# Shifting the split weight tiles by 0, 64, 128 or 192 bytes, and four raw buffers instead of five

## The chip, the cores and the metric

The kernel runs on one core of one Trainium2 chip. The metric is the device time of one execution in microseconds (us). Before the change the median of three runs is 472.22 us, from 471.35 to 472.73.

## The reference

One decoder layer for 256 tokens of width 2048, all in float32. `x` is normalized, multiplied by a weight `w_in` (2048 x 8192), and the product is cut into eight groups of 1024 columns. Four of them feed a gated convolution of width 3, four feed attention with 8 heads of 128. The two results are normalized, gated, joined and multiplied by `w_out` (2048 x 2048).

```
h = rms_norm(x, norm_gain)
proj = einsum('bsd,de->bse', h, w_in)
h_conv, b_gate, c_gate, z_conv, q, k, v, z_attn = split(proj, ...)
y_conv = rms_norm(short_gated_conv(h_conv, b_gate, c_gate, conv_w), conv_out_gain) * silu(z_conv)
y_attn = rms_norm(moba_attention(rms_norm(q), rms_norm(k), v), attn_out_gain) * silu(z_attn)
x = x + einsum('bse,ed->bsd', concat([y_conv, y_attn]), w_out)
```

With 256 tokens there is one attention block, so the attention is plain causal attention inside it.

## The kernel before

**Split weights.** A float32 weight is used as a sum of two parts in a 32-bit type that TensorE takes in one pass (`float32r`): the high part is the rounded weight, the low part what is left. For each piece of weights, ScalarE writes the high part `wh` from the loaded tile `raw` (line 465), then VectorE writes the low part `wl` as `raw - wh` (line 466). `x`, `y` and the parts of attention are split in the same way. A product is three products of parts (high x high, high x low, low x high), which `by_parts` (line 103) issues as three matmuls.

**Pieces.** The weights are cut into 160 pieces of 512 KB, 1024 numbers in each of 128 partitions, and there are three kinds:

- A: 6 units of 8 pieces each for q, k, v. A piece holds 2 rows of 512 columns. The weight part is the moving operand, and 128 tokens of `xs` are the stationary one. 12 matmuls of 512 columns a piece (lines 106 to 108).
- B: 20 units of 4 pieces for the gates and the convolution. A piece holds 4 rows of 256 columns. The weight part is the stationary operand (128 columns at a time), and `xs` is the moving one: high weights meet both parts of `x` in one matmul of 512 columns (line 473), low weights the high part alone in one of 256 (line 474). 8 such pairs a piece.
- Y: 8 units of 4 pieces for `w_out`. The weight part moves, `yh` and `yl` are stationary. 12 matmuls of 512 columns a piece; the last unit (4 pieces) is cut into 18 smaller matmuls a piece, 6 of 512 and 12 of 256 columns, into `aux` accumulators.

**Order.** The main loop (line 514) goes over the pieces in the order A, B, Y. At piece j it issues the load of piece j + 6 (line 447, SyncE's queue), the split of piece j + 3 and the matmuls of piece j, then the small work that is due. Every engine runs its instructions in this order. `raw`, `wh` and `wl` have 5 buffers each (line 52), so SyncE's load of piece j waits until VectorE has read `raw` of piece j - 5, and ScalarE's split of piece j waits until TensorE has done the matmuls of piece j - 5. The first four pieces are loaded and split by halves (lines 442, 458, 459), beside them the 16 rows of `xT` (line 162). Attention runs beside the later A pieces and the earlier B pieces. Its score matmuls (line 253) take `yh` and `yl`, its output matmuls (lines 298, 299) take `vh` and `vl` as stationary operands and `pTh`, `pTl` as moving ones; transposes (lines 223, 283) go through TensorE as well, with `ident` as the moving operand.

**Where the tiles lie.** The allocator puts the tiles one after another. In the built program they begin at these bytes of each partition: `xs` 17408, `yh` 50176, `yl` 66560, `wh` 120832 + 4096 n, `wl` 141312 + 4096 n, `raw` 100352 + 4096 n, `t2k` 161792 + 2048 n, all multiples of 1024 (two `pad` tiles, lines 64 and 314, take up what is left over before them). Of the other operands `ident` (84800), `vh` (202048 + 2048 n), `vl` (206144 + 2048 n) and `qk_0` (193856 + 2048 n) lie 64 bytes past a multiple of 256, `rxb` (86880) lies 96 past one, `p` (219008 + 1536 n) 128 past one, and `pTh` (223744 + 1024 n) and `pTl` (225792 + 1024 n) lie on one.

Of the kernel before, what the change touches and what calls it, by code (L numbers as in the profile page):

```python
# [10 lines left out]
F32 = mybir.dt.float32  # L11
FR = mybir.dt.float32r
# [5 lines left out]
P = 128  # L18
SEQ = 256
NT = SEQ // P  # L20
DM = 2048
KT = DM // P
DG = 1024
CW = 512
# [17 lines left out]
LEAD = 3  # L42
# [6 lines left out]
def hybrid_layer(ctx: ExitStack, tc: tile.TileContext, xT, x, w_a, w_b, w_out, par, out):  # L49
    nc = tc.nc  # L50
    cst = ctx.enter_context(tc.tile_pool(name="cst", bufs=1))
    wp = ctx.enter_context(tc.tile_pool(name="wp", bufs=LEAD + 2))
# [106 lines left out]
    def load_xT(k, n):  # L159
        if k % 2 == 0:  # L160
            x_raw[k // 2] = t2k((P, 2, SEQ))
        nc.sync.dma_start(x_raw[k // 2][:, k % 2:k % 2 + n], xT[:, k:k + n])  # L162
        if k == 0:
            nc.sync.dma_start(prm, par)

    def split_x(k):
        src, g = x_raw[k // 2][:, k % 2], prm[:, G_IN + k:G_IN + k + 1]
        nc.scalar.activation(xs[:, k, 0], src, AF.Copy, scale=g)  # L168
        nc.vector.scalar_tensor_tensor(xs[:, k, 1], src, g, xs[:, k, 0].bitcast(F32), op0=OP.mult, op1=OP.subtract)
# [259 lines left out]
    pieces = []  # L429
    for kind, n, w, kts in units:  # L430
        pk, cols = (4, GW) if kind == "B" else (2, CW)
        pieces += [(kind, n, w[:, k:k + pk], k, k + pk == kts, pk, cols) for k in range(0, kts, pk)]
    raws, ws = {}, {}

    def load(j):
        if j >= len(pieces):
            return
        _, _, src, _, _, pk, cols = pieces[j]
        raw = raws[j] = wp.tile([P, pk, cols], F32, name="raw")
        if j < SINGLE:  # L440
            for i in range(2):
                nc.sync.dma_start(raw[:, i:i + 1], src[:, i:i + 1])  # L442
                load_xT(2 * j + i, 1)
            return
        if j < KT // 2:
            load_xT(2 * j, 2)
        nc.sync.dma_start(raw, src)

    def split(j):
        if j >= len(pieces):  # L450
            return
        raw = raws.pop(j)
        wh = wp.tile(list(raw.shape), FR, name="wh")
        wl = wp.tile(list(raw.shape), FR, name="wl")
        ws[j] = (wh, wl)
        if j < SINGLE:
            for i in range(2):
                nc.scalar.activation(wh[:, i], raw[:, i], AF.Copy)
                nc.vector.tensor_tensor(wl[:, i], raw[:, i], wh[:, i].bitcast(F32), op=OP.subtract)
                split_x(2 * j + i)  # L460
            return
        if j < KT // 2:
            for i in range(2):
                split_x(2 * j + i)
        nc.scalar.activation(wh, raw, AF.Copy)  # L465
        nc.vector.tensor_tensor(wl, raw, wh.bitcast(F32), op=OP.subtract)  # L466
# [42 lines left out]
    for j in range(LOADS):  # L509
        load(j)  # L510
    for j in range(LEAD):
        split(j)
    acc = None
    for j, (kind, n, _, k, last, pk, _) in enumerate(pieces):
        load(j + LOADS)
        split(j + LEAD)
        if k == 0:
            acc = ps.tile([P, 2, CW], F32, name="acc", bufs=2)
# [14 lines left out]
        else:  # L533
            n, k0 = n
# [62 lines left out]
```

## Time and profile before

| | |
|---|---|
| median of 3 runs | 472.22 us (471.35 to 472.73) |
| profiled execution, its own time | 470.43 us |
| its span, first to last instruction | 468.7 us |
| TensorE matmul busy | 462.6 us, 99% |
| TensorE weight load busy | 394.6 us, 84% |
| VectorE busy | 303.9 us, 65% |
| ScalarE busy | 242.6 us, 52% |
| matmuls | 2416 |
| DMA | 90.63 MB, mean 193 GB/s |

The busy time of a matmul counts from its start to its modelled end, and neighbours overlap, so the spacing of starts in the timeline says more than the duration. PE is TensorE, PEld its weight loads, DVE VectorE, ACT ScalarE, POOL GpSimd, SPq the queue of SyncE. Lines are those of the kernel before.

### The profile page before, as it was taken

The page shows a single profiled execution, that of the slowest core. Times are in us where ns is not written, and L with a number is a line of the kernel's source. Part 1 is how long each engine was busy: PE and PEld are TensorE (multiplying, and loading weights), DVE is VectorE, ACT ScalarE, POOL GpSimd, SP SyncE. Part 2 cuts the span into 40 slices and gives each one's busy share as a digit, 9 for nine tenths or more (in the row PEclk, how much of TensorE's full clock was granted, in tenths as well). Part 3 has the DMA queues.
Part 4 walks back from the last instruction along what each step waited for, and adds up shares of the span by engine and source line. Part 5 has one row for each costly group of instructions (what it writes and reads, how often), then busy time and mean ns, then how long its engine had stood idle before and what let it go on. Part 6 is the DMA issues. An engine that isn't in the chain of part 4 may idle for free.

```text
span 468.7 us, 6428 instructions
## 1 busy us (share of the span) xinstructions
PE 462.6 (99%) x2416; PEld 394.6 (84%) x2416; DVE 303.9 (65%) x440; ACT 242.6 (52%) x337; POOL 20.1 (4%) x23
## 2 busy tenths in 40 slices
PE   8999999999999999999999999999999999999996
PEld 5788888888888888888888888888888888888885
DVE  5988767567475666678866675666666676566541
ACT  6975546465536667656545544455544553343320
POOL 1002200002020000000100000000000010000100
PEclk9999999999999999999999999999999999999999
DMA  8987664645665555555565556656655778766611
GB/s 256 392 258 244 206 211 140 191 136 170 180 196 162 181 172 153 166 187 179 185 206 184 188 180 190 202 185 187 199 191 175 219 238 259 246 187 201 219 67 47
DMA packets 27583, 90.63 MB, mean 193 GB/s; under 512 B 3232, under 2 KB 4512, under 8 KB 27552
## 3 DMA queue, kind: packets, MB, share of 16 engines
q1 hardware_dynamic: 27072, 88.65, 59.9%
q0 software_dynamic: 480, 1.57, 1.0%
q8 instruction: 19, 0.31, 0.3%
q14 instruction: 12, 0.10, 0.1%
HBM read 88.11 MB, written 2.10 MB: 192 GB/s over the span
## 4 chain that ended last, share of the span: by engine, by line
PE 95%; DMA 2%; SPq 1%; DVE 0%; ACT 0%; issue 0%
PE acc L473 31%; PE acc L474 16%; PE acc L107 14%; PE acc L108 14%; PE acc L106 14%; PE aux L107 1%; PE aux L106 1%; PE aux L108 1%; DMA raw<-in_w_a_dram 1%; DMA t2k<-in_xT_dram 1%; PE aux L223 1%; PE aux L283 1%; SPq L442 0%; PE aux L252 0%; PE aux L299 0%; SPq L162 0%
## 5 line engine op out<-in xcount | busy, mean ns | idle before, releaser
L466 DVE TENSOR_TENSOR wl<-raw,wh 128x1024 fp32r<-128x1024 f32 x156 | 190.3, 1223 | 99.5 <-ACT wh L465 99.1
L473 PE MATMUL acc<-xs,wh 128*128 128x512 f32 x640 | 223.4, 393 | 0.0
L465 ACT ACTIVATE wh<-raw 128x1024 fp32r<-128x1024 f32 x156 | 164.6, 1057 | 111.4 <-PE acc L108 59.5
L474 PE MATMUL acc<-xs,wl 128*128 128x256 f32 x640 | 179.1, 280 | 0.0
L473 PEld LDWEIGHTS acc<-xs,wh 128*128 128x128 f32 x640 | 119.9, 187 | 26.9
L474 PEld LDWEIGHTS acc<-xs,wl 128*128 128x128 f32 x640 | 120.9, 189 | 0.0
L106 PE MATMUL acc<-wh,xs 128*128 128x512 f32 x192 | 76.3, 397 | 0.4 <-ACT xs L168 0.4
L107 PE MATMUL acc<-wl,xs 128*128 128x512 f32 x192 | 75.1, 391 | 0.4 <-DVE wl L466 0.4
L108 PE MATMUL acc<-wh,xs 128*128 128x512 f32 x192 | 75.1, 391 | 0.0
L107 PE MATMUL acc<-wl,yh 128*128 128x512 f32 x112 | 43.6, 389 | 0.0
L108 PE MATMUL acc<-wh,yl 128*128 128x512 f32 x112 | 43.6, 389 | 0.0
L106 PE MATMUL acc<-wh,yh 128*128 128x512 f32 x112 | 43.6, 389 | 0.0
L106 PEld LDWEIGHTS acc<-wh,xs 128*128 128x128 f32 x192 | 36.3, 189 | 8.3 <-ACT xs L168 1.3
L107 PEld LDWEIGHTS acc<-wl,xs 128*128 128x128 f32 x192 | 36.4, 189 | 7.8 <-DVE wl L466 0.8
L108 PEld LDWEIGHTS acc<-wh,xs 128*128 128x128 f32 x192 | 36.2, 188 | 7.7
L338 ACT ACTIVATE t2k<-acc 128x512 f32<-128x512 f32 x20 | 11.9, 596 | 28.5 <-PE acc L474 28.5
L339 DVE TENSOR_TENSOR t2k<-acc,t2k 128x512 f32<-128x512 f32 x20 | 13.8, 691 | 18.1 <-ACT t2k L338 18.1
L106 PEld LDWEIGHTS acc<-wh,yh 128*128 128x128 f32 x112 | 21.0, 188 | 4.4
L108 PEld LDWEIGHTS acc<-wh,yl 128*128 128x128 f32 x112 | 21.0, 188 | 4.3
L107 PEld LDWEIGHTS acc<-wl,yh 128*128 128x128 f32 x112 | 21.0, 188 | 4.3
L308 ACT ACTIVATE yh<-t2k,prm 128x256 fp32r<-128x256 f32 x16 | 7.3, 503 | 16.6 <-DVE t2k L374 16.6
L111 POOL TENSOR_TENSOR r<-ms,neg_half 128x8 f32<-128x8 f32 x4 | 10.1, 2525 | 78.6 <-DVE ms L210 78.6
(117 smaller groups left out, 289.3 us busy)
## 6 DMA issues: line engine op xcount, KB each, us to landing
raw<-in_w_b_dram SPq DMA_DIRECT2D x80, 512.0 KB, 4.6
raw<-in_w_a_dram SPq DMA_DIRECT2D x44, 512.0 KB, 3.9
raw<-in_w_out_dram SPq DMA_DIRECT2D x32, 512.0 KB, 3.8
raw<-in_w_a_dram SPq DMA_DIRECT2D x8, 256.0 KB, 4.1
t2k<-in_x_dram SPq DMA_DIRECT2D x8, 256.0 KB, 4.8
out_dram<-t2k POOLq DMA_DIRECT2D x6, 256.0 KB, 3.4
t2k<-in_xT_dram SPq DMA_DIRECT2D x8, 128.0 KB, 4.1
t2k<-in_xT_dram SPq DMA_DIRECT2D x4, 256.0 KB, 5.6
```

Source lines behind the costliest of these rows:

```text
L106: nc.tensor.matmul(acc, sh, mh, start=first, stop=False)
L107: nc.tensor.matmul(acc, sh, ml, start=False, stop=False)
L108: nc.tensor.matmul(acc, sl, mh, start=False, stop=last)
L111: nc.gpsimd.tensor_tensor(dst, ms, neg_half[:, :ms.shape[-1]], op=OP.pow)
L223: nc.tensor.transpose(a[:, i * P:(i + 1) * P], qn[key, t][:, i], ident)
L308: nc.scalar.activation(yh[:, kt + i], src, AF.Copy, scale=g)
L338: nc.scalar.activation(d, acc[:, :, SEQ:], AF.Copy)
L339: nc.vector.tensor_add(d, acc[:, :, :SEQ], d)
L465: nc.scalar.activation(wh, raw, AF.Copy)
L466: nc.vector.tensor_tensor(wl, raw, wh.bitcast(F32), op=OP.subtract)
L473: nc.tensor.matmul(acc[:, b], wh, xs[:, k].rearrange("p s t -> p (s t)"), start=first, stop=False)
L474: nc.tensor.matmul(acc[:, b, :SEQ], wl, xs[:, k, 0], start=False, stop=last)
```

## The change

The tiles `wh` and `wl` become 64 floats (256 bytes) longer, and the part of 1024 numbers that is used begins 0, 16, 32 or 48 floats (0, 64, 128 or 192 bytes) into the tile. The offset is chosen by `half`, a running number of half units: 0 to 11 in the A pieces (4 pieces each), 0 to 39 in the B pieces (2 pieces each), 12 to 27 in the Y pieces (2 pieces each). The high part takes offset `half % 4`, the low part `half // 4 % 4`, so that 16 halves in turn go through all pairs. `raw` has 4 buffers instead of 5. Since a buffer of `wh` or `wl` is now 4352 bytes long and `raw` takes 4096 bytes less, the buffers of the two begin at different multiples of 256, and everything behind them moves down by 1536 bytes.

```diff
-        raw = raws[j] = wp.tile([P, pk, cols], F32, name="raw")
+        raw = raws[j] = wp.tile([P, pk, cols], F32, name="raw", bufs=LEAD + 1)
...
-        wh = wp.tile(list(raw.shape), FR, name="wh")
-        wl = wp.tile(list(raw.shape), FR, name="wl")
+        kind, n, _, k, _, pk, cols = pieces[j]
+        half = 2 * n + k // (KT // 2) if kind != "Y" else 12 + 2 * (n[0] + (0 if n[1] else DM // CW)) + k // (KT // 4)
+
+        wh, wl = (wp.tile([P, 2 * CW + 64], FR, name=m)[:, o:o + 2 * CW].rearrange("p (k c) -> p k c", k=pk)
+                  for m, o in (("wh", half % 4 * 16), ("wl", half // 4 % 4 * 16)))
```

## Rows read from the trace of the kernel before

**Rows 1.** The page's totals of each engine (busy us, share of the span, instructions) and, from its 40 equal slices, the clock that was granted to TensorE in tenths.
```profile
PE 462.6 (99%) x2416; PEld 394.6 (84%) x2416; DVE 303.9 (65%) x440; ACT 242.6 (52%) x337; POOL 20.1 (4%) x23
PEclk9999999999999999999999999999999999999999
```

**Rows 2.** The chain that ended last: its shares of the span by line.
```profile
PE acc L473 31%; PE acc L474 16%; PE acc L107 14%; PE acc L108 14%; PE acc L106 14%; PE aux L107 1%; PE aux L106 1%; PE aux L108 1%; DMA raw<-in_w_a_dram 1%; DMA t2k<-in_xT_dram 1%; PE aux L223 1%; PE aux L283 1%; SPq L442 0%; PE aux L252 0%; PE aux L299 0%; SPq L162 0%
```

**Rows 3.** The page's groups of instructions: line, engine, operation, tiles, shapes, count | busy us, mean ns of one | idle us before them and what ended most of it.
```profile
L466 DVE TENSOR_TENSOR wl<-raw,wh 128x1024 fp32r<-128x1024 f32 x156 | 190.3, 1223 | 99.5 <-ACT wh L465 99.1
L473 PE MATMUL acc<-xs,wh 128*128 128x512 f32 x640 | 223.4, 393 | 0.0
L465 ACT ACTIVATE wh<-raw 128x1024 fp32r<-128x1024 f32 x156 | 164.6, 1057 | 111.4 <-PE acc L108 59.5
```

**Rows 4.** The timeline of TensorE: start us, duration us, engine, line, operation; first an A stretch of 27 steps, then a Y stretch of 27 steps.
```profile
129.81 0.39 PE L106 MATMUL acc<-wh,xs 128*128 128x512 f32 x1
...
135.93 0.39 PE L106 MATMUL acc<-wh,xs 128*128 128x512 f32 x1
...
409.62 0.39 PE L106 MATMUL acc<-wh,yh 128*128 128x512 f32 x1
...
415.74 0.39 PE L106 MATMUL acc<-wh,yh 128*128 128x512 f32 x1
```

**Rows 5.** The same view in two B stretches: 20 pairs from 213.65 to 220.72, and 17 pairs from 249.80 to 255.69. Then stretches of the B pieces for line 473 alone: length, busy us and count of its matmuls and of its weight loads, granted clock, DMA share, GB/s.
```profile
213.65 0.40 PE L473 MATMUL acc<-xs,wh 128*128 128x512 f32 x1
...
220.72 0.40 PE L473 MATMUL acc<-xs,wh 128*128 128x512 f32 x1
...
249.80 0.39 PE L473 MATMUL acc<-xs,wh 128*128 128x512 f32 x1
...
255.69 0.39 PE L473 MATMUL acc<-xs,wh 128*128 128x512 f32 x1
...
200.00:220.00 20.00, 20.00 (x57) 10.62 (x57) 1.00 0.55 176
220.00:376.00 156.00, 155.81 (x451) 84.01 (x450) 1.00 0.61 192
```

**Rows 6.** The timeline of TensorE in attention: the first of three matmuls of 256 columns with `vh`, `vl` as the stationary operand and the one that follows the three, then two score matmuls of 256 columns.
```profile
172.21 0.28 PE L106 MATMUL aux<-pTh,vh 128*128 128x256 f32 x1
...
172.57 0.38 PE L299 MATMUL aux<-pT,v 128*128 128x128 f32 x2
...
173.46 0.28 PE L107 MATMUL aux<-yl,yh 128*128 128x256 f32 x1
173.58 0.28 PE L108 MATMUL aux<-yh,yl 128*128 128x256 f32 x1
```

**Rows 7.** Groups by form of ScalarE and VectorE: writes of 512 numbers into `vh` and into `yh`, into `vl` and into `yl`.
```profile
L382 ACT ACTIVATE vh<-acc,rx 128x512 fp32r<-128x512 f32 x2 | 1.4, 690 | 1.3 <-PE acc L108 1.3
L244 ACT ACTIVATE yh<-aux,prm 128x512 fp32r<-128x512 f32 x6 | 4.1, 684 | 4.1 <-PE aux L223 4.1
L383 DVE SCALAR_TENSOR_TENSOR vl<-acc,rx,vh 128x512 fp32r<-128x512 f32 x2 | 1.5, 747 | 0.6 <-ACT vh L382 0.6
L245 DVE SCALAR_TENSOR_TENSOR yl<-aux,prm,yh 128x512 fp32r<-128x512 f32 x6 | 4.5, 752 | 6.7 <-ACT yh L244 6.7
```

**Rows 8.** What SyncE's queue waited for longest (us in total, times, longest us); then the timeline around a load in the steady part, the landing of that load (KB, us from issue), and ScalarE's split of the same piece.
```profile
SPq L447 <- DVE wl L466: 291.1, 123, 5.2
...
413.63 1.23 DVE L466 TENSOR_TENSOR wl<-raw,wh 128x1024 fp32r<-128x1024 f32 x1 [1.27 <-ACT wh L465]
414.89 0.33 SPq L447 DMA_DIRECT2D raw<-in_w_out_dram  x1
...
raw<-in_w_out_dram SPq DMA_DIRECT2D x1, 512.0 KB, 3.5
...
426.14 1.06 ACT L465 ACTIVATE wh<-raw 128x1024 fp32r<-128x1024 f32 x1 [1.66 <-PE acc L108]
```

**Rows 9.** The start: the timeline's loads of pieces 8, 9, 11 and 12, under those of 8, 11 and 12 the landing (KB, us from issue); then ScalarE's split of piece 8, TensorE's first matmul with the low part of piece 8, ScalarE's split of piece 11 and VectorE's subtraction for it.
```profile
14.60 0.44 SPq L447 DMA_DIRECT2D raw<-in_w_a_dram  x1
raw<-in_w_a_dram SPq DMA_DIRECT2D x1, 512.0 KB, 8.5
17.75 0.33 SPq L447 DMA_DIRECT2D raw<-in_w_a_dram  x1
...
22.89 0.33 SPq L447 DMA_DIRECT2D raw<-in_w_a_dram  x1
raw<-in_w_a_dram SPq DMA_DIRECT2D x1, 512.0 KB, 4.9
25.61 0.33 SPq L447 DMA_DIRECT2D raw<-in_w_a_dram  x1
raw<-in_w_a_dram SPq DMA_DIRECT2D x1, 512.0 KB, 4.3
...
23.84 1.05 ACT L465 ACTIVATE wh<-raw 128x1024 fp32r<-128x1024 f32 x1
...
28.81 0.39 PE L107 MATMUL acc<-wl,xs 128*128 128x512 f32 x1
28.95 1.04 ACT L465 ACTIVATE wh<-raw 128x1024 fp32r<-128x1024 f32 x1
...
32.09 1.22 DVE L466 TENSOR_TENSOR wl<-raw,wh 128x1024 fp32r<-128x1024 f32 x1
```

## The prediction

> **What bounds the kernel now.** I read the page's totals first, then the chain of waits, then the groups of instructions. TensorE is busy for 99% of the span at a granted clock of 1.00, the upper of its two levels (2.4 GHz), in every slice [rows 1, 5]; the chain that ended last is 31 + 16 + 14 + 14 + 14 = 89% matmuls into `acc` [rows 2]. ScalarE and VectorE, which make the split weights, are busy for 52% and 65%, and in front of the large splits ScalarE stands idle 111.4 us, VectorE 99.5 us, mostly for a tile that TensorE has still to free [rows 3]. So the time is the number of matmuls times the spacing of their starts, and an edit counts only if it changes that spacing or lets TensorE wait.
>
> The busy time of a matmul (393 ns on line 473 [rows 3]) overlaps its neighbours', so I took spacings from the timeline. In the A stretch, where a weight tile is the moving operand, 27 steps take 135.93 - 129.81 = 6.12 us: 226.7 ns each. The Y stretch gives 27 steps in 415.74 - 409.62 = 6.12 us, the same [rows 4]. In the B stretch, where the weight tile is stationary, a pair (512 and 256 columns) has two spacings: 17 pairs in 255.69 - 249.80 = 5.89 us are 346.5 ns, but 20 pairs in 220.72 - 213.65 = 7.07 us are 353.5 ns [rows 5]. At 2.4 GHz 512 columns take 213.3 ns and 768 take 320 ns, so every matmul carries some 13.3 ns that is not columns, and a pair in the slower pattern 7 ns more.
>
> **The offsets, B stretch (1280 matmuls, weights stationary).** Before, every split weight, `xs`, `yh` and `yl` begin at multiples of 1024 bytes, so no row shows a large matmul with a shifted weight. The nearest are in attention: `vh` and `vl` lie 64 bytes past a multiple of 256 and are the stationary operands of three matmuls with 256 columns of `pTh` or `pTl`, which begin on one; from 172.21 to 172.57 they are 120 ns each. With both operands aligned, line 107 of the scores at 173.46 is followed at 173.58, also 120 ns [rows 6]. A shift of the stationary operand is thus costed at 0. Its bounds: above, pairs that ran fast take the slow pattern's 7 ns. From 220 us on TensorE was in the fast one: 451 of the line 473 matmuls in 156 us are one per 346 ns, against 57 in the 20 us before, one per 351 [rows 5]. 451 x 7 ns = 3.2 us; with all 640 it could not pass 4.5. Below, three of four matmuls lose their 13.3 ns: 960 x 13.3 = 12.8 us. Zero is nearest to the rows, since they show a shifted operand of this very kind.
>
> **The offsets, A and Y stretches (weights moving).** 48 pieces x 12, 28 x 12 and 4 x 18 are 984 matmuls; with three of four offsets not zero, 738 have a shifted moving operand. For that there is no row of 256 or 512 columns; the identity (64 bytes off) moves in the transposes, but only for 128 columns. Bounds: above, each takes the 7 ns that separate the two patterns of the B pair, 738 x 7 = 5.2 us; below, each loses its 13.3 ns, 738 x 13.3 = 9.8 us. I take 0, by the row of the shifted stationary operand: what may collide is a position of one operand against the other, and there a difference of 64 bytes changed nothing. This is the weaker half of the argument.
>
> **The offsets, the writers.** The splits write to shifted addresses: ScalarE into `vh` (64 off) 690 ns against 684 into aligned `yh`, VectorE into `vl` (64 off) 747 ns against 752 into aligned `yl` [rows 7]. At most 1% of 1057 ns, 10 ns a piece, in front of idle time of the same engine [rows 3]: 0. The same instructions are issued, of the same shapes; none is added. If that cover were gone, 160 x 10 ns = 1.6 us.
>
> **Four raw buffers.** SyncE's load of piece j waited for the subtraction of piece j - 5, and now waits for that of j - 4, one piece later; behind it in SyncE's queue stand only later loads. In the steady part: the load issued at 414.89 followed the subtraction of 413.63 + 1.23 us and landed 3.5 us later, 418.4. Its own split comes five pieces of 2.72 us after that subtraction, at 427.2 on VectorE and 426.14 on ScalarE, so some 7.7 us of slack stand against a shift of 2.7 us [rows 8]: 0. If this slack went, TensorE would still have three finished pieces ahead.
>
> At the start it is tighter. The load of piece 8, issued at 14.60, moves one subtraction later, to 17.75, where that of piece 9 stood; it landed 8.5 us after issue, at 23.1, and one issued at 25.61 with less ahead of it took 4.3 us [rows 9]. So it was mostly queued, and lands between 17.75 + 4.3 = 22.1, which would be no delay, and 26.2, if the whole shift of 3.15 us is passed on. Even then ScalarE's split begins at 26.2 instead of 23.84, the subtraction ends at 26.2 + 1.06 + 1.22 = 28.5, and TensorE wants the first low part of piece 8 at 28.81 [rows 3, 9]. Piece 11's load moves from 22.89 to 25.61; with 4.3 us it lands at 29.9, 1.0 us after ScalarE began that split, but VectorE, which is behind, begins the subtraction only at 32.09 [rows 9]. So 0, with 0 to 1 us as bounds: what is late next is VectorE, and it has the same order of work as before. SyncE's waits, 291.1 us for these subtractions [rows 8], stay, since only their place moves.
>
> **Sum.** 0 + 0 + 0 + 0. The profiled execution took 470.43 us (span 468.7 and 1.7 around it); its forecast is 470.4. The median of the runs is 472.22, 1.8 us above, and I forecast 472.2 for it.
>
> **Rivals.**
> (1) *The slow pattern becomes the rule* (slower). Mechanism: a weight tile that begins off the old grid puts loading and streaming out of step, as in the stretch of 353.5 ns, and the offset changes every two pieces of B before the fast pattern can hold. For it: both patterns exist in one kernel with the same addresses, and the slow one lasted over many pieces, so it is easily entered. Against it: the 120 ns steps of `vh`. Price: 3.2 us in B, 475.4; with the moving operands of A and Y too, 3.2 + 5.2 = 8.4 us, 480.6. It decides from 200 pairs on (200 x 7 ns = 1.4 us).
> (2) *A shift takes away part of the 13.3 ns* (faster). For it: that part is fixed per matmul, equal for 256 and 512 columns (120 - 106.7 and 226.7 - 213.3), and all operands of these matmuls begin at the same place of 1024 bytes. Against it: the 120 ns steps show it undiminished at 64 bytes. Price: moving operands alone 9.8 us, 462.4; half of that 467.3.
> The Trainium skill's page "TensorE: Matmul & The Clock Gate" (Back-to-back issue gap) gives columns / 2.4 GHz + about 2.5 ns, 215.8 ns here, for matmuls that follow each other. This case's 226.7 ns does not agree; by that rule some 10.9 ns would be there to be won, an estimate of 738 x 10.9 = 8.0 us or 464.2 us.
> (3) *The buffers bite at the start* (slower): pieces 8 to 11 come late and TensorE waits once, 1 us, 473.2: still within what can be told. For it the 0.3 us that are left for piece 8 in the worst case; against it the 8.5 us, most of them queue.
> (4) *The offsets don't act*: were the tiles rounded so that the slices begin on the old grid again, nothing would move; same time as the forecast.
>
> **How the numbers follow.** About 0.3%, 1.4 us, can be told from no change. Forecast with (3) and (4), no change: 0.53. (1): 0.32, as the moving operand's shift is unseen and the slow pattern is at hand. (2): 0.15. Faster and slower are the chances of (2) and (1). The likeliest case's own range is 470.8 to 473.6. The range for 8 in 10 takes all of it and most of (1), up to 478.5, and the near edge of (2), down to 469.5.
>
> **What would show it.** Right: in the changed kernel's timeline the A and Y steps stay at 226.7 ns and the B pairs at 346.5 ns in every half stretch, whatever its two offsets; SyncE's loads wait for the subtraction of the piece four before, and no split of ScalarE's waits for a raw tile after 40 us. Wrong: spacings that change where the half changes, in one direction for the same offset; A and Y changing and B not would say that the moving operand's start matters; B pairs at 353 ns far behind the last attention matmul would be rival 1; a step under 220 ns rival 2; idle time of TensorE between 28 and 40 us rival 3.

## The result and the profile after

The changed kernel takes 476.51 us (median of three runs, 476.39 to 477.0) against 472.22 before: a ratio of 1.0096 with a 95% interval of 1.007 to 1.0123. It is slower by 4.3 us by the medians, 4.5 us by the ratio. The forecast was no change.

The page of the changed kernel: its totals, the chain by line, two groups of matmuls and the two splits (line numbers above 452 are 3 higher than before; columns as in [rows 1 to 3]).
```profile
PE 467.1 (98%) x2416; PEld 394.4 (83%) x2416; DVE 303.7 (64%) x440; ACT 242.5 (51%) x337; POOL 20.1 (4%) x23
...
PE acc L476 31%; PE acc L477 16%; PE acc L107 14%; PE acc L108 14%; PE acc L106 14%; DMA raw<-in_w_a_dram 2%; PE aux L106 1%; PE aux L107 1%; PE aux L108 1%; PE aux L223 1%; PE aux L283 1%; PE aux L252 0%; PE aux L299 0%; SPq L162 0%; SPq L442 0%; DVE wl L469 0%
...
L469 DVE TENSOR_TENSOR wl<-raw,wh 128x1024 fp32r<-128x1024 f32 x156 | 190.2, 1223 | 103.7 <-ACT wh L468 102.9
L476 PE MATMUL acc<-xs,wh 128*128 128x512 f32 x640 | 224.5, 394 | 0.0
L468 ACT ACTIVATE wh<-raw 128x1024 fp32r<-128x1024 f32 x156 | 164.5, 1057 | 116.8 <-PE acc L108 57.0
...
L106 PE MATMUL acc<-wh,yh 128*128 128x512 f32 x112 | 44.1, 394 | 0.0
```
The chain is still matmul behind matmul; the one new entry, VectorE's split, rounds to 0%. The splits take exactly what they took, 1057 and 1223 ns [rows 3]. The mean duration of a matmul rises by 1 ns in B, and by 5 ns in Y (389 before): the duration runs to a modelled end, so it only hints at the spacing.

Where the time went is read from the starts of four matmuls in the timeline of TensorE: of the first of piece 5, the first of B, the first of Y and the first of the last piece. Before:
```profile
20.42 0.39 PE L106 MATMUL acc<-wh,xs 128*128 128x512 f32 x1
...
147.75 0.39 PE L473 MATMUL acc<-xs,wh 128*128 128x512 f32 x1
...
376.68 0.39 PE L106 MATMUL acc<-wh,yh 128*128 128x512 f32 x1
...
461.57 0.40 PE L106 MATMUL aux<-wh,yh 128*128 128x512 f32 x1
```
After:
```profile
21.64 0.40 PE L106 MATMUL acc<-wh,xs 128*128 128x512 f32 x1
...
151.03 0.39 PE L476 MATMUL acc<-xs,wh 128*128 128x512 f32 x1
...
381.00 0.40 PE L106 MATMUL acc<-wh,yh 128*128 128x512 f32 x1
...
467.55 0.39 PE L106 MATMUL aux<-wh,yh 128*128 128x512 f32 x1
```
A from piece 5 on grew from 127.33 to 129.39 us (2.06), B from 228.93 to 229.97 (1.04), Y from 84.89 to 86.55 (1.66): together 4.8 us, about what the medians show. The start is 1.22 us later in this profile; it is taken up with the first experiment.

The same view inside half stretches of the changed kernel: an A piece at offsets 192/0 (high/low bytes), two Y pieces at 0/0 and at 192/0, and two B pieces of 8 pairs each, the last one at 0/0 and the first one at 64/0 behind it. Last come 24 Y steps at 64/64.
```profile
44.09 0.40 PE L106 MATMUL acc<-wh,xs 128*128 128x512 f32 x1
...
46.68 0.39 PE L108 MATMUL acc<-wh,xs 128*128 128x512 f32 x1
...
406.19 0.39 PE L106 MATMUL acc<-wh,yh 128*128 128x512 f32 x1
...
408.91 0.40 PE L106 MATMUL acc<-wh,yh 128*128 128x512 f32 x1
...
422.83 0.40 PE L106 MATMUL acc<-wh,yh 128*128 128x512 f32 x1
...
425.64 0.39 PE L106 MATMUL acc<-wh,yh 128*128 128x512 f32 x1
...
249.66 0.40 PE L476 MATMUL acc<-xs,wh 128*128 128x512 f32 x1
...
252.49 0.39 PE L476 MATMUL acc<-xs,wh 128*128 128x512 f32 x1
...
255.21 0.39 PE L476 MATMUL acc<-xs,wh 128*128 128x512 f32 x1
...
431.20 0.40 PE L106 MATMUL acc<-wh,yh 128*128 128x512 f32 x1
...
436.80 0.40 PE L106 MATMUL acc<-wh,yh 128*128 128x512 f32 x1
```
The A steps are (46.68 - 44.09) / 11 = 235 ns, the Y steps 226.7 at 0/0, 2.81 / 12 = 234 at 192/0 and 5.60 / 24 = 233.3 at 64/64: in these stretches with shifted weights the steps are longer than the 226.7 ns of [rows 4]. B pairs take 2.83 / 8 = 353.8 ns at 0/0, though nothing is shifted there, and 2.72 / 8 = 340.0 at 64/0, which is less than either pattern of [rows 5]. So the offset matters, and it is not all that matters.

### The profile page after: what moved, and what is told of

Same layout as the page of the kernel before. It is cut to its first block, busy times and chain, and to the rows that moved or that the text cites. A ratio compares the mean times of both kernels' runs of the same rounds, so it can differ in the third digit from the quotient of the medians.

```text
span 474.6 us, 6427 instructions
## 1 busy us (share of the span) xinstructions
PE 467.1 (98%) x2416; PEld 394.4 (83%) x2416; DVE 303.7 (64%) x440; ACT 242.5 (51%) x337; POOL 20.1 (4%) x23
## 4 chain that ended last, share of the span: by engine, by line
PE 95%; DMA 2%; SPq 1%; DVE 0%; ACT 0%; issue 0%; DVEq 0%
PE acc L476 31%; PE acc L477 16%; PE acc L107 14%; PE acc L108 14%; PE acc L106 14%; DMA raw<-in_w_a_dram 2%; PE aux L106 1%; PE aux L107 1%; PE aux L108 1%; PE aux L223 1%; PE aux L283 1%; PE aux L252 0%; PE aux L299 0%; SPq L162 0%; SPq L442 0%; DVE wl L469 0%
## 5 line engine op out<-in xcount | busy, mean ns | idle before, releaser
L469 DVE TENSOR_TENSOR wl<-raw,wh 128x1024 fp32r<-128x1024 f32 x156 | 190.2, 1223 | 103.7 <-ACT wh L468 102.9
L468 ACT ACTIVATE wh<-raw 128x1024 fp32r<-128x1024 f32 x156 | 164.5, 1057 | 116.8 <-PE acc L108 57.0
```

## The experiments

**Theories.** O: the offsets cost it all, through where weights begin against the tiles that they meet. R: the four raw buffers cost the start. Of O there are two forms: each operand's place counts by itself (A), or the difference of the two operands' places (D). And it may be the change of offset, not the offset (C). (These letters name theories, not kinds of pieces.) The first four kernels bear on them.

**Four raw buffers alone.**
```diff
-        raw = raws[j] = wp.tile([P, pk, cols], F32, name="raw")
+        raw = raws[j] = wp.tile([P, pk, cols], F32, name="raw", bufs=LEAD + 1)
```


> Four raw buffers, nothing else; every split weight still begins at a multiple of 1024 bytes. Theory O (the offsets cost all of it, by where a weight tile begins against the tiles that it meets): 472.2 us as before, within 1.4 us; A and Y steps 226.7 ns, fast B pairs 346.5 ns, TensorE at piece 5 near 20.4 us. Theory R (four buffers cost the start): TensorE reaches piece 5 near 21.6 us as in the changed kernel, and the time is 1.2 us up, 473.4 us. If all of the change were the buffers: 476.5 us.

Measured 471.61 us against 471.57, ratio 1.0004 (0.9989 to 1.0018). TensorE's first matmul of piece 5, and what ScalarE waited for transfers between 20 and 468 us, in this kernel:
```profile
20.44 0.39 PE L106 MATMUL acc<-wh,xs 128*128 128x512 f32 x1
...
ACT wh L465 <- DMA raw<-in_w_a_dram: 3.7, 3, 1.6
```
The time is as before and so is the start (20.42), so R falls. The start scatters between profiles: in those of all kernels here piece 5 begins at 20.42 to 21.16 us with five buffers and at 20.44 to 22.37 with four, and the second kernel, which begins it at 21.85, takes no longer. So the 1.22 us of the changed kernel's profile are not shown to be the buffers'; by the second kernel's interval four buffers, with the longer tiles, cost 0.5 us at most. The splits do wait for the later loads, three times and up to 1.6 us, and TensorE waits for nothing in that stretch of this trace.

**The longer tiles with all offsets 0** (the changed kernel with `half % 4 * 0` and `half // 4 % 4 * 0`).

> The changed kernel with all offsets at 0: the tiles stay 256 bytes longer, so the buffers begin at different multiples of 256 bytes, and four raw buffers stay. Theory O: 472.2 us, or 473.4 us with theory R's start; A and Y steps 226.7 ns. Theory G (multiples of 256 bytes are already off the grid that counts): 474 to 476.5 us, with steps of 229 to 234 ns in A and Y that differ from buffer to buffer.

Measured 471.6 us, ratio 1.0001 (0.9991 to 1.0011). Buffers that begin at other multiples of 256 bytes are as good as those at multiples of 1024. With this the whole loss is the offsets'.

**Everything moved by 64 bytes.**
```diff
-    cst.tile([P, 224], F32, name="pad_front")
+    cst.tile([P, 240], F32, name="pad_front")
```


> The kernel before with everything from xs on moved by 64 bytes: weights, xs, yh and yl all begin 64 bytes past a multiple of 1024, five raw buffers. Theory A (the place of one operand by itself counts, each operand that begins off the grid pays): A and Y steps near 233 ns, 984 x 6.5 ns = 6.4 us up from there alone, 478 us or more. Theory D (the difference of the places of the two operands counts): nothing changes, 472.2 us, steps of 226.7 and 346.5 ns.

Measured 471.43 us, ratio 1.0006 (0.9986 to 1.0026). Pairs of B and steps of Y in this kernel's timeline (20 pairs, 24 steps):
```profile
299.88 0.39 PE L473 MATMUL acc<-xs,wh 128*128 128x512 f32 x1
...
306.81 0.39 PE L473 MATMUL acc<-xs,wh 128*128 128x512 f32 x1
...
410.13 0.39 PE L106 MATMUL acc<-wh,yh 128*128 128x512 f32 x1
...
415.57 0.39 PE L106 MATMUL acc<-wh,yh 128*128 128x512 f32 x1
```
6.93 / 20 = 346.5 and 5.44 / 24 = 226.7 ns. Every operand begins 64 bytes off, and nothing changes. Theory A falls. The writers of the weights wrote to shifted places here too, so they are not the cause either.

**Only the weights (and what lies behind them) moved by 64 bytes.**
```diff
-    cst.tile([P, 24], F32, name="pad_end")
+    cst.tile([P, 40], F32, name="pad_end")
```


> The kernel before with raw, wh, wl and all behind them moved by 64 bytes, xs, yh and yl where they were: one pair of offsets, 64 and 64, for the whole kernel, five raw buffers. Theories A and D: A and Y steps of 229.5 to 233.5 ns (3 to 7 ns x 984 = 3 to 6.5 us up) and B pairs of 352 to 353 ns (6 ns x 640 = 3.8 us, less 1.2 us that are lost already), so 477 to 481 us. Theory C (it is the change of the offset every few pieces that throws TensorE into the slow pattern): steps return to 226.7 and 346.5 ns, 472.2 us.

Measured 476.71 us, ratio 1.0104 (1.0085 to 1.0124). The same stretches of this kernel, and steps of 256 columns at the end of Y (19 pairs, 21 steps, 10 steps); then the four starts that divided the span above:
```profile
299.94 0.40 PE L473 MATMUL acc<-xs,wh 128*128 128x512 f32 x1
...
306.66 0.40 PE L473 MATMUL acc<-xs,wh 128*128 128x512 f32 x1
...
409.64 0.39 PE L106 MATMUL acc<-wh,yh 128*128 128x512 f32 x1
...
414.45 0.39 PE L106 MATMUL acc<-wh,yh 128*128 128x512 f32 x1
...
468.77 0.28 PE L107 MATMUL aux<-wl,yh 128*128 128x256 f32 x1
...
469.90 0.28 PE L108 MATMUL aux<-wh,yl 128*128 128x256 f32 x1
...
21.16 0.39 PE L106 MATMUL acc<-wh,xs 128*128 128x512 f32 x1
...
149.68 0.39 PE L473 MATMUL acc<-xs,wh 128*128 128x512 f32 x1
...
381.92 0.39 PE L106 MATMUL acc<-wh,yh 128*128 128x512 f32 x1
...
467.28 0.39 PE L106 MATMUL aux<-wh,yh 128*128 128x512 f32 x1
```
6.72 / 19 = 353.7 ns a pair, 4.81 / 21 = 229.0 ns a step of 512 columns, but 1.13 / 10 = 113 ns a step of 256 (120 before). The time is at the low end of what was expected of A and D. D stands, and C falls as the only cause, since a single offset that never changes costs about as much as the whole rotation. But it does so in other places: by the four starts the A stretch is 1.2 us longer than before, Y 0.5 us, and B 232.24 - 228.93 = 3.3 us, with the slower pattern throughout, where the rotation lost 2.06, 1.66 and 1.04. That the two totals are alike is chance. And at the same 64/64 a Y step took 233.3 ns in the changed kernel and 229.0 here, so in Y, too, the pair of offsets alone does not set the step; how much of the rotation's loss comes from the changes themselves stays open. The difference of places can also shorten a step, as the 256-column steps show.

**The parts of the change by stretch.** The changed kernel with its offsets in A and Y alone (both multiplied by `kind != "B"`), and in B alone (by `kind == "B"`).

> The changed kernel's offsets in A and Y, 0 in B. By the spacings of the changed kernel's trace A loses 2.1 us and Y 1.6 us against before, and B returns to 346.7 ns: 3.7 us up, 475.0 us on the 471.3 of before on this chip. Rival (B carries the loss): 472 us.

> The changed kernel's offsets in B, 0 in A and Y. By the changed kernel's trace B loses 1.1 us: 472.4 us on 471.3, and A and Y are back at 226.7 ns. Rival (B carries the loss): 475 us.

A and Y alone: 476.11 us on 471.78, ratio 1.0083 (1.0063 to 1.0104), 3.9 us by the ratio and 4.3 by the medians. In its trace A is 2.1 us and Y 1.6 us longer than before, and B as long as before. B alone: 472.68, ratio 1.0011 (0.9996 to 1.0026), 0.5 us by the ratio and 0.9 by the medians, which can't be told from nothing; its trace has B 0.8 us longer than before. Some four fifths of the changed kernel's loss are the moving weights'.

**64/0 in all of B.** This takes up the 340.0 ns seen in the changed kernel. From here on offsets are chosen in the changed kernel's code:
```diff
+        oh, ol = (16, 0) if kind == "B" else (0, 0)
...
-                  for m, o in (("wh", half % 4 * 16), ("wl", half // 4 % 4 * 16)))
+                  for m, o in (("wh", oh), ("wl", ol)))
```


> Offsets 64 (high) and 0 (low) for all B pieces, 0 and 0 in A and Y. In the changed kernel that pair of offsets ran at 340.0 ns a pair in two half stretches (entered from the slow pattern of 353.3) and at 350 in one (entered from the fast pattern). Theory N (the pair of offsets alone sets the spacing, the attention matmuls between disturbed the one): 340.0 ns from the last attention piece on at the latest, 55 to 80 pieces x 8 x 6.67 ns = 2.9 to 4.3 us, and up to 1.2 us more if the disturbed pieces gain too: 467 to 469 us. Theory P (what ran before sets which pattern is held): entered from the fast pattern it stays at 350 ns, 80 pieces x 28 ns = 2.2 us up less 1.2 us lost before: 472.5 to 474 us.

Measured 467.53 us on 471.33, ratio 0.992 (0.9892 to 0.9947): faster than both kernels. Two B stretches of it, 14 pairs before and 21 behind the last interruption of B by other matmuls:
```profile
207.90 0.40 PE L477 MATMUL acc<-xs,wh 128*128 128x512 f32 x1
...
212.85 0.40 PE L477 MATMUL acc<-xs,wh 128*128 128x512 f32 x1
...
299.84 0.39 PE L477 MATMUL acc<-xs,wh 128*128 128x512 f32 x1
...
306.98 0.39 PE L477 MATMUL acc<-xs,wh 128*128 128x512 f32 x1
```
4.95 / 14 = 353.6 ns, then 7.14 / 21 = 340.0, with the same offsets. The time fits theory N (the offsets alone set the spacing); the two stretches don't: the offset alone does not set it.

**Does a disturbance last?** All offsets 0, but one half stretch at 192/192: `oh, ol = (48, 48) if kind == "B" and half == 20 else (0, 0)`.

> All offsets 0 but one half stretch of B (two pieces, half 20, after the last attention matmul) at 192 and 192. Theory P: behind it the pairs stay at 353.3 ns to the end of B, 38 pieces x 53 ns = 2.0 us up, 473.6 us. Theory N: the two pieces cost 0.1 us and the next pairs are back at 346.7 ns, 471.6 us.

Measured 473.72 us, ratio 1.0046 (1.0025 to 1.0067). Pairs ahead of the odd half stretch (20) and long behind it (21):
```profile
255.78 0.39 PE L477 MATMUL acc<-xs,wh 128*128 128x512 f32 x1
...
262.71 0.39 PE L477 MATMUL acc<-xs,wh 128*128 128x512 f32 x1
...
299.65 0.40 PE L477 MATMUL acc<-xs,wh 128*128 128x512 f32 x1
...
307.07 0.40 PE L477 MATMUL acc<-xs,wh 128*128 128x512 f32 x1
```
346.5 ns, then 7.42 / 21 = 353.3. Two pieces out of 80 put TensorE into the slower pattern, and it stays there though all offsets are 0 again. N falls; P (what ran before sets which pattern is held) stands.

**64/0 entered in another way, and a mix.** The first has 0/0 up to half 15 with 192/192 at half 14, then 64/0. The second has 64/0 in B, but 192/64 in halves 7 to 11, and 64/64 in the last four pieces of Y.

> As the kernel with 64 and 0 in B, but all offsets 0 up to half 13, then one half stretch at 192/192, one at 0/0, and 64/0 from half 16 on: the order in which the changed kernel came to 340.0 ns. Theory P: 48 pieces x 53 ns = 2.6 us less, plus 0.2 us for the two halves: 469.2 us, also if the kernel with 64/0 throughout stays at 350 ns. Theory N: the same 340.0 ns here as there.

> As the kernel with 64/0 in B, but half stretches 7 to 11 of B (where that kernel sat at 353 ns behind the last attention matmul) at 192/64, which the changed kernel ran at 346.7 ns there, and the last four pieces of Y at 64/64, whose 256-column matmuls ran at 113.3 instead of 120 ns in the kernel with all weights at 64. Theory P: 10 pieces x 53 ns + 4 pieces x 80 ns = 0.9 us less than the kernel with 64/0 alone, 466.7 us, if 64/0 is entered again as 340.0 ns at half 12; 470.5 us if it is entered as 350 ns (56 pieces x 80 ns = 4.5 us back, less 0.9).

Measured 473.05 us, ratio 1.003 (1.0012 to 1.0048), and 471.72 us, ratio 0.9996 (0.9983 to 1.0009). 20 pairs at 64/0 in the first; the second has the same 7.00 us for 20 pairs in this stretch:
```profile
299.67 0.40 PE L477 MATMUL acc<-xs,wh 128*128 128x512 f32 x1
...
306.67 0.40 PE L477 MATMUL acc<-xs,wh 128*128 128x512 f32 x1
```
350.0 ns, held to the end of B. That the order slow pattern, then 64/0, brings 340.0 is refuted: what ran before decides, but "fast" or "slow" does not name what about it does. The mix shows what that is worth: by its offsets it was to be the best of all, and it gives back the whole gain. Nor did its last four pieces of Y repeat the 113 ns at 64/64: their 256-column steps took about 118 ns.

**A search with finer steps**, measured once, 474.21 us: 8 pieces for each offset.
```diff
+        tries = ((16, 0), (8, 0), (4, 0), (24, 0), (0, 8), (12, 0), (8, 8))
+        if kind == "B":
+            oh, ol = tries[half // 4 - 3] if half >= 12 else (0, 0)
+        else:
+            oh = ol = (4, 8, 12, 24)[half // 4 - 3] if kind == "Y" else 0
```


> A search, one look: in B, from the last attention matmul on, each pair of offsets for 8 pieces: 64/0, 32/0, 16/0, 96/0, 0/32, 48/0, 32/32 bytes (high/low); in Y, each for 8 pieces, 16, 32, 48, 96 bytes for both; A at 0. Theory D (any difference of places that isn't the old one shifts the spacing): B pairs between 340 and 354 ns, changing with the offset, and Y steps above 226.7 ns for each. If only multiples of 64 bytes count: 16, 32 and 48 bytes run like 0, at 346.7 and 226.7 ns.

38 pairs at 64/0, 23 at 0/32, then Y steps at 16 and at 32 bytes (27 and 24 steps):
```profile
229.81 0.39 PE L481 MATMUL acc<-xs,wh 128*128 128x512 f32 x1
...
242.73 0.39 PE L481 MATMUL acc<-xs,wh 128*128 128x512 f32 x1
...
312.90 0.40 PE L481 MATMUL acc<-xs,wh 128*128 128x512 f32 x1
...
320.88 0.39 PE L481 MATMUL acc<-xs,wh 128*128 128x512 f32 x1
...
382.05 0.40 PE L106 MATMUL acc<-wh,yh 128*128 128x512 f32 x1
...
388.31 0.39 PE L106 MATMUL acc<-wh,yh 128*128 128x512 f32 x1
...
405.02 0.39 PE L106 MATMUL acc<-wh,yh 128*128 128x512 f32 x1
...
410.62 0.39 PE L106 MATMUL acc<-wh,yh 128*128 128x512 f32 x1
```
340.0 and 347.0 ns a pair, 231.9 and 233.3 ns a step. None of the other pairs of offsets in B ran below 346 ns. Already 16 bytes lengthen the Y step, and none of the four shortens it.

## Why the prediction was wrong

- **A and Y, the term that failed.** The step "I take 0, by the row of the shifted stationary operand" cost the forecast. Measured alone it is 3.9 us (A and Y with offsets, B without); its upper bound, 5.2 us, held for the sum, though the steps at 192/0 are 8 ns longer and not 7. The row was too coarse: three steps at a resolution of 10 ns [rows 6] can hardly show the 4 ns a step that make 3.9 us out of 984 matmuls, and 1.4 us, the least that counts, is 1.4 ns a step. And it showed another case, a shifted stationary operand with 256 columns; in the fourth kernel, moving operands of 256 columns at 64 bytes went the other way, to 113 ns.
- **"What may collide is a position of one operand against the other"** was right (third and fourth kernel), but the row behind "there a difference of 64 bytes changed nothing" did not carry over to the large matmuls. The Trainium skill's page "TensorE: Matmul & The Clock Gate" (Step-by-step: what each phase is for) says that weights are loaded through a read port of their own and take no read bandwidth from the running matmul. Here the spacing depends on the difference of the two operands' places, 226.7 to 229.0 ns with one shift of 64 bytes, so the two are not independent in time; what holds a step up, no run here shows.
- **B, 0 as well**, measured 0.8 to 1.0 us by the traces: within its bounds of -12.8 and 3.2, and alone not told from nothing. It came near 0 by luck, as a sum of both signs: in the changed kernel's trace 64/0 gains and 64/64 loses up to 6.7 ns a pair. A constant offset shows that B is not indifferent: 3.3 us lost in the fourth kernel, 3.8 us won with 64/0.
- **The writers, 0**: right, 1057 and 1223 ns unchanged.
- **Four buffers, 0**: right in time (first kernel). The sign I named was wrong: splits do wait for transfers after 40 us (5.1 us in 3 waits in the changed kernel, the longest 1.8), and the three finished pieces hide it. The prediction looked at pieces 8 and 11 and not at 16 to 18.
- **Rival 1** had the direction, and its mechanism in part. Its lower price, 475.4 us, is near by luck: that is the price of B, and here A and Y carry the loss. The change of offset is not needed, since a constant one costs about as much, and there is no one slow pattern. What it priced for B, 3.2 us, did come out in the fourth kernel (3.3 us, 353.7 ns a pair), under a constant offset. That a pattern holds until something disturbs it, the one odd half stretch shows. Its chance of 0.32 was too low: an unseen operand in 984 matmuls on the critical path, with bounds of 5.2 us up and 9.8 us down, deserved more than the row that I put in its place.
- **Rival 2** was real, in one pair of offsets: 340.0 ns against 346.5, and 467.53 us when all of B takes it. That this is near its price of 467.3 us is luck: the price was for moving weights, of which no stretch of 512 columns that is shown here got shorter. Its premise that all operands begin at the same place of 1024 bytes does not hold for the slices: every second stationary slice begins 512 bytes past such a place, and the steps of [rows 4] are alike all the same. The rotation has it in 3 of its 40 half stretches, and one of those ran at 350.

## What to carry to other kernels

Where TensorE is the bound, the places of the two operands of a matmul, one against the other, are worth a trial: moving all weight tiles by 64 bytes cost 1% here, and moving the high parts alone by 64 bytes in B gave 0.8% in one kernel and none in two others. Compute how small an effect per instruction would already count, and don't take a row as evidence of zero whose resolution is coarser. Measure such a layout as a whole and in place: what a half stretch runs at depends on what ran before it, and gains read from parts did not add up.

## What the runs showed of the hardware

- The spacing of 512-column matmuls with these operands was 226.7 ns in steady stretches at equal places, 229.0 in one kernel and 233.3 in another at 64 bytes of difference, and up to 235 at 192/0; moving both operands by 64 bytes (226.7 ns, ratio 1.0006) or the weight buffers by multiples of 256 (ratio 1.0001) changed nothing.
- A pair of B runs in patterns that repeat over many pieces: 340.0, 346.5, 350.0 and 353.3 ns were all seen, 346.5 and 353.3 with the same offsets, 340.0 and 350.0 (and 353.6) with the same other ones. A disturbance of two pieces changed the pattern for the 38 that followed. What chooses the pattern stays open.
